# Conditioning rows of up to eight weight chunks summed into one tile and turned into columns four times

## The chip, the cores and the metric

The kernel runs on one core of one Trainium2 chip. The metric is the device time of one execution in microseconds. Engines: PE is TensorE (matmul), PEld its weight load, DVE VectorE, ACT ScalarE, POOL GpSimd, SP SyncE, which here issues the weights' DMAs.

## What is computed

A sequence of 256 tokens with 1024 features goes through a first block (attention, a state-space mixer and a linear recurrence side by side) and then through two decoder layers. Each decoder layer has a front (retention, an RWKV recurrence and a short convolution, merged by gates) and an experts' half (32 experts, two of them chosen for each token). All is float32. The part that matters here is the conditioning of the two decoder layers: one vector `c` of 1024 numbers gives, per layer, six vectors of 1024 by which the layer shifts, scales and gates its activations:

```python
mod = silu(c) @ w_ada[l] + b_ada[l]          # 1024 x 6144, for both layers
h = modulate(rms_norm(x), shift, scale)      # h * (1 + scale) + shift
x = x + gate * branch                        # once for the front, once for the experts
```

## The kernel before

All weights come in chunks of 128x4096 float32 (2 MB), in one fixed order of use that `order` (L399) writes down. `w_ada` is 24 of those chunks, 12 per layer, each for 512 of the 6144 columns; they are set between the other chunks: (0,0) to (0,8) in block 1, (0,9) to (0,11) and (1,0) to (1,4) in the front of layer 0, (1,5) to (1,11) in the front of layer 1. A chunk is written (l,i): layer and number.

SBUF is one large tile, `memory`, and a second one, `parts` (split operands) or `spare` (expert chunks). `Plan` (L224) makes a dry run first, notes at which step each tile and chunk is taken and freed, gives each its columns, and lets each chunk's DMA start as early as its place is free, but in the order of use; `start` (L420) issues it on SP. The chunks' times count steps of the program (a taking or a freeing), so code that takes fewer tiles shifts the table.

Dense projections take float32 weights in two parts: `unit` (L519) makes a high part of 1024 weights per partition on ACT (L522) and a low part on DVE (L523), and `mm3` (L527) multiplies them. Their PE work stands in the profile as `pst<-parts` or `po<-parts`, L505, since one helper `mm` issues nearly all matmuls. A chain of small steps (recurrence, attention, softmax) is written between pieces of dense work by `weave` (L664); the order in which each engine gets its instructions is then set by the tile framework's scheduler, not by the source's order alone.

The conditioning: `spread_c` (L1058) sets silu(c) as the first of 32 columns of a zeroed tile `cs32`. `ada` (L1090) gets a chunk and multiplies it in eight matmuls with 32 weight columns: four partial rows, each a quarter of the features, stand in partitions 0, 32, 64 and 96 of one PSUM bank, with zeros in the others. DVE copies the bank to a tile `r` (L1100). A closure `columns` (L1104) is set aside in `self.side`; `flush` (L1119) runs what waits there at the next `unit` or the next `ada`. It turns the row into columns with the features on partitions: `r`'s slices are the weights and a column of ones is the moving operand, which sums the four partial rows as well. Vectors 3 and 4 (shift and scale of the experts' half) are wanted in another order of features and take every eighth column of `r`, in eight matmuls for 64 partitions each; the others take four matmuls for 128. DVE then adds the bias (L1111 or L1115).

```python
for j in range(8):                                            # vectors 3 and 4
    self.mm(q[o, j:j + 1], r[:, j::8], one, True, True)
...
for j in range(4):                                            # the others
    self.mm(q[:, j:j + 1], r[:, j * 128:(j + 1) * 128], one, True, True)
```

At the end of block 1, `add_x` (L594) adds the sums to x, `inv_rms` (L614) makes the rows' rs with three Newton steps on DVE (L583 to L585), `scale_x` (L621) scales x by it, and `flip` (L628) transposes it on PE (L631) for the front. In an expert's half, chunks for gate, up and down projection (`in_weg`, `in_weu`, `in_wed`) are used in turn.

Of the kernel before, what the change touches and what calls it, by code (L numbers as in the profile page):

```python
# [21 lines left out]
# ---------------------------------------------------------------- host layout  # L22
# [5 lines left out]
def _chunk(w):  # L28
    """[K*128, N] -> [128, K*N], row d = 128*k + p at partition p."""
    kp, n = w.shape  # L30
    return w.reshape(kp // 128, 128, n).transpose(1, 0, 2).reshape(128, -1)


def _rows(v):
    return np.broadcast_to(np.asarray(v).reshape(1, -1), (128, np.asarray(v).size))
# [24 lines left out]
def _constants():  # L60
# [6 lines left out]
    c.add("io32", _rows(np.arange(33, dtype=np.float32)))  # L67
    c.add("io9", _rows(np.arange(8, dtype=np.float32) - 9.0))
# [32 lines left out]
def _layout(inp):  # L101
# [44 lines left out]
    for l in range(2):  # L146
# [19 lines left out]
        lay["ada"].append(np.stack([_chunk(ada[:, i * 512:(i + 1) * 512]) for i in range(12)]))  # L166
# [25 lines left out]
# ---------------------------------------------------------------- the kernel  # L192
class Act:
    """Activations, features on partitions: float32 and its exact two-part split."""
# [5 lines left out]
class Dry:  # L200
    """Stands for anything in the run that only plans the memory."""
# [22 lines left out]
class Plan:  # L224
    """Sizes and lifetimes of all tiles by a dry run, and from them each tile's place and each weight chunk's time to
    start: as early as there is room for it. Times count the steps of the program that take or free memory."""
# [19 lines left out]
    def place(self, first):  # L246
        """An address for every tile, from the bottom, and for every chunk while it is used, from the top: the large
        and long ones first, and before them those that found no room."""
# [28 lines left out]
    def early(self):  # L277
        """Every chunk in turn starts as early as some place is free for it, in the main part or, while that is open
        for chunks, in the other."""
# [26 lines left out]
class Memory:  # L306
    """Columns of one tile, given out and taken back in the order of the program; the waits follow from the data."""
# [6 lines left out]
    def step(self):  # L314
        """One step on; the chunks whose time has come start."""
# [6 lines left out]
    def new(self, *sh, p=128, part=0):  # L322
        """A tile of this shape on the first p partitions."""
# [22 lines left out]
    def chunk(self):  # L346
        """The next weight chunk's number."""
        self.step()
        if self.tiles is None:
            self.plan.chunks.append([Plan.CHUNK, self.now, None, 0])  # L350
        self.got += 1
        return self.got - 1
# [6 lines left out]
    def turn(self, key, *sh, bufs=2, p=128, part=0):  # L359
        """One of bufs tiles of this shape, by turns, until done()."""  # L360
# [11 lines left out]
class Kernel:  # L372
# [26 lines left out]
    def order(self):  # L399
        """The weight chunks in the order in which they are used."""  # L400
# [19 lines left out]
    def start(self, n, t):  # L420
# [4 lines left out]
        # an expert half's last chunk in parts, so that little work is left after the last of them  # L425
# [6 lines left out]
    def get(self, *key, k=8, hold=False):  # L432
        """The next weight chunk; it is there until the next call, or until drop()."""
# [20 lines left out]
    def run(self, plan, dry):  # L454
# [24 lines left out]
        # the last norm: all but the last quarter times its gain before the rows' rs is there  # L479
# [7 lines left out]
    # -- helpers  # L487
    def turn_part(self, spare):
        """The second part of the memory is for split operands, or it is spare and takes weight chunks."""
# [14 lines left out]
    def mm(self, out, lhsT, rhs, start, stop):  # L504
        self.nc.tensor.matmul(out, lhsT=lhsT, rhs=rhs, start=start, stop=stop)  # L505

    def psb(self, tag="sm", name="pst"):
        """A bank of PSUM."""
        return self.ps.tile([128, 512], F, tag=tag, bufs=BANKS[tag], name=name)

    def split(self, f, n=4):
        """f = hi + lo, both exact in the tensor engine's one-pass float32."""
# [6 lines left out]
    def unit(self, src, a, n=1024):  # L519
        """The split of 1024 weights a partition."""  # L520
# [6 lines left out]
    def mm3(self, jobs, left):  # L527
        """out += w.T @ a, or a.T @ w, for every out, w, a, start, stop, from the parts: those with the weights' high
        part first. The product of both low parts is below float32's own rounding."""
# [6 lines left out]
    def fm_pair(self, w, act, m, K=8):  # L536
        """Feature tiles m, m+1 of the projection of act, features on partitions."""
# [10 lines left out]
    def tm(self, w, act):  # L548
        """The projection of act, tokens on partitions: two banks of 128 tokens."""
# [8 lines left out]
    def tm_out(self, w, act, accs, first, last):  # L558
        """accs[t][h] += the projection of four feature tiles of act."""
# [9 lines left out]
    def rsqrt(self, out, in_, scale, eps, tmp):  # L569
        """out = (in_*scale + eps) ** -0.5 on small tiles."""  # L570
# [3 lines left out]
    def newton(self, out, v):  # L574
        """out = v ** -0.5: a first guess from the bits, then three Newton steps; v is overwritten."""
# [11 lines left out]
    def squares(self, t, h):  # L587
        """The mean square of half a row of x, into ss."""
# [5 lines left out]
    def add_x(self, accs, last=False):  # L594
        """x += accs, and its mean squares."""
# [9 lines left out]
    def last_gain(self):  # L605
        """The last norm's gain on every partition."""
# [18 lines left out]
    def flip(self, v, by8, use):  # L625
        """Two feature tiles of v's transpose at a time: use(k, their bank)."""
# [7 lines left out]
    def norm_T(self, gain, shift=None):  # L634
        """The split of x's rms-norm, transposed: uT[d, t] * gain[d] (+ shift[d])."""
# [28 lines left out]
    def weave(chain, dense):  # L664
        """Trace the steps of a chain with pieces of dense work between them."""
# [4 lines left out]
    # -- block 1  # L670
    def block1(self):
# [10 lines left out]
        def softplus(out, x, t):  # L682
            """out = max(x, 0) + log1p(exp(-|x|)); t: four scratch tiles."""
# [15 lines left out]
        # forget gates and time steps, heads on partitions  # L699
# [19 lines left out]
        # token-major dt, exp(cumsum), decay to the chunk's end  # L719
# [14 lines left out]
        def conv(p, raw, out, j, wn, bn, nt):  # L734
            """causal conv of width 4 of psum tile p along time."""
# [1257 lines left out]
```

## Time and profile before

| what | value |
|---|---|
| runs | 1982.15, 1986.38, 1988.5 us; median 1986.38 |
| profiled execution, span from first to last instruction | 1985.8 us (its time is not listed apart from this) |
| PE busy | 1659.6 us, 84% |
| DVE busy | 958.3 us, 48% |
| ACT busy | 557.6 us, 28% |
| DMA, mean | 295 GB/s, 586.13 MB |
| chain that ended last | DMA 19%, PE 3%, all others together under 1% of the span |

Each share is a mean over stages of different kinds. The chain that ended last reaches back only into the last experts' half, so what ends the earlier stages is read from the stages themselves. Busy PE is not PE at its peak: its matmuls are pipelined and their ends modelled, so what an instruction costs is read here from start to start. A float32 matmul of the program stands as two matmuls in the trace, one with the split operands as one.

### The profile page before, as it was taken

The page shows a single profiled execution, that of the slowest core. Times are in us where ns is not written, and L with a number is a line of the kernel's source. Part 1 is how long each engine was busy: PE and PEld are TensorE (multiplying, and loading weights), DVE is VectorE, ACT ScalarE, POOL GpSimd, SP SyncE. Part 2 cuts the span into 40 slices and gives each one's busy share as a digit, 9 for nine tenths or more (in the row PEclk, how much of TensorE's full clock was granted, in tenths as well). Part 3 has the DMA queues.
Part 4 walks back from the last instruction along what each step waited for, and adds up shares of the span by engine and source line. Part 5 has one row for each costly group of instructions (what it writes and reads, how often), then busy time and mean ns, then how long its engine had stood idle before and what let it go on. Part 6 is the DMA issues. An engine that isn't in the chain of part 4 may idle for free. (4 is left out here: it accounts for less than half of the span.)

```text
span 1985.8 us, 42525 instructions
## 1 busy us (share of the span) xinstructions
PE 1659.6 (84%) x18982; PEld 1379.8 (69%) x18982; DVE 958.3 (48%) x2013; ACT 557.6 (28%) x856; POOL 76.6 (4%) x54
## 2 busy tenths in 40 slices
PE   6999999999999887776677599999988877667774
PEld 6877669788988765555455398889987765545553
DVE  7896556788438433222222456784376332222222
ACT  6835444524425300000000235244253100000001
POOL 0001000000004000000000000000040000000000
PEclk9999999999989899888888799999998998788888
DMA  8654563563325799999999953642258999999996
GB/s 344 236 193 155 201 262 131 212 251 132 128 100 234 291 426 426 426 427 425 427 427 426 399 221 133 259 161 105 109 188 324 391 426 425 427 426 426 426 426 252
DMA packets 43119, 586.13 MB, mean 295 GB/s; under 512 B 4816, under 2 KB 5456, under 8 KB 7984
## 3 DMA queue, kind: packets, MB, share of 16 engines
q1 hardware_dynamic: 41904, 579.72, 71.6%
q0 software_dynamic: 1024, 3.61, 0.5%
q8 instruction: 151, 2.47, 0.5%
q14 instruction: 40, 0.33, 0.0%
HBM read 582.26 MB, written 1.05 MB: 294 GB/s over the span
## 5 line engine op out<-in xcount | busy, mean ns | idle before, releaser
L505 PE MATMUL pst<-parts 128*128 128x256 f32 (+2 forms) x4344 | 636.6, 306 | 17.1 <-DVE parts L523 12.4
L505 PEld LDWEIGHTS pst<-parts 128*128 128x128 f32 (+1 forms) x4344 | 578.7, 197 | 65.8 <-issue 17.7
L505 PE MATMUL pst<-memory 128*32 128x256 f32 (+11 forms) x5152 | 519.7, 354 | 83.6 <-DMA memory<-in_wed_dram 43.5
L505 PEld LDWEIGHTS pst<-memory 128*32 128x32 f32 (+5 forms) x5152 | 373.7, 157 | 189.2 <-issue 115.9
L505 PE MATMUL pst<-memory,spare 128*32 128x128 f32 (+1 forms) x6848 | 266.1, 317 | 136.1 <-DMA memory<-in_weu_dram 77.4
L523 DVE TENSOR_TENSOR parts<-memory,parts 128x1024 fp32r<-128x1024 f32 (+1 forms) x233 | 296.7, 1276 | 156.6 <-ACT parts L522 147.6
L522 ACT ACTIVATE parts<-memory 128x1024 fp32r<-128x1024 f32 (+1 forms) x233 | 245.6, 1057 | 425.0 <-PE pst L505 348.1
L505 PEld LDWEIGHTS pst<-memory,spare 128*32 128x32 f32 (+1 forms) x6848 | 237.4, 129 | 178.8 <-issue 117.7
L1886 DVE TENSOR_TENSOR spare<-pst,memory 32x256 f32<-32x256 f32 x256 | 107.6, 420 | 172.0 <-PE pst L505 169.1
L1870 ACT ACTIVATE memory<-pst 128x128 f32<-128x128 f32 x64 | 25.2, 393 | 544.7 <-PE pst L505 525.9
L1872 DVE TENSOR_TENSOR memory<-memory,pst 128x128 f32<-128x128 f32 x64 | 24.0, 375 | 193.8 <-PE pst L505 193.7
L1871 DVE TENSOR_TENSOR memory<-memory,pst 128x128 f32<-128x128 f32 x64 | 24.2, 378 | 193.3 <-ACT memory L1870 193.3
L505 PE MATMUL po<-parts 128*128 128x512 f32 x384 | 89.6, 392 | 2.0 <-ACT parts L515 1.5
L505 PEld LDWEIGHTS po<-parts 128*128 128x128 f32 x384 | 71.5, 188 | 20.6 <-ACT parts L515 3.0
L1822 ACT ACTIVATE spare<-pst,memory,gain 128x128 f32<-128x128 f32 x64 | 29.3, 457 | 189.0 <-DVE spare L1824 189.0
L505 PE MATMUL pst<-spare 128*32 128x128 f32 x1408 | 51.0, 304 | 25.9 <-DMA spare<-in_weu_dram 12.9
L505 PEld LDWEIGHTS pst<-spare 128*32 128x32 f32 x1408 | 45.4, 123 | 32.8 <-issue 26.2
L505 PE MATMUL acc<-spare,memory 128*128 128x512 f32 x128 | 59.8, 610 | 9.2 <-DVE spare L1886 9.2
L1824 DVE TENSOR_SCALAR spare<-pst,gain,memory 128x128 f32<-128x128 f32 x64 | 26.2, 409 | 66.1 <-PE pst L505 56.7
L1291 POOL TENSOR_TENSOR memory<-memory 128x1024 f32<-128x1024 f32 x16 | 47.8, 3019 | 209.8 <-ACT memory L1145 209.8
L505 PEld LDWEIGHTS acc<-spare,memory 128*128 128x128 f32 x128 | 21.8, 189 | 38.1 <-DVE spare L1886 22.8
L505 PE MATMUL pst<-spare,memory 128*32 128x256 f32 x352 | 27.4, 459 | 14.5 <-DMA spare<-in_wed_dram 8.5
(381 smaller groups left out, 974.1 us busy)
## 6 DMA issues: line engine op xcount, KB each, us to landing
memory<-in_weg_dram SPq DMA_DIRECT2D x54, 2048.0 KB, 39.1
memory<-in_weu_dram SPq DMA_DIRECT2D x52, 2048.0 KB, 39.3
memory<-in_wed_dram SPq DMA_DIRECT2D x52, 2048.0 KB, 39.1
memory<-in_w_dram SPq DMA_DIRECT2D x33, 2048.0 KB, 8.6
memory<-in_ada_dram SPq DMA_DIRECT2D x24, 2048.0 KB, 7.6
memory<-in_wg_dram SPq DMA_DIRECT2D x12, 2048.0 KB, 8.2
spare<-in_weu_dram SPq DMA_DIRECT2D x12, 2048.0 KB, 39.1
spare<-in_wed_dram SPq DMA_DIRECT2D x10, 2048.0 KB, 40.5
```

The costliest lines, as they stand in the source:

```text
L505: self.nc.tensor.matmul(out, lhsT=lhsT, rhs=rhs, start=start, stop=stop)
L522: self.nc.scalar.activation(hi, src, AF.Copy)
L523: self.nc.vector.tensor_tensor(lo, src, hi.bitcast(F), op=OP.subtract)
L1291: nc.gpsimd.tensor_tensor(w[:, k], w[:, k], gb, op=OP.mult)
L1822: A.activation(XG[:, j + i, :], p[:, i, :], AF.Identity, scale=gain(j + i), bias=shift(j + i))
L1824: V.tensor_scalar(XG[:, j + i, :], p[:, i, :], gain(j + i), shift(j + i), op0=OP.mult, op1=OP.add)
L1870: A.activation(hf, pg, AF.Sigmoid)
L1871: V.tensor_tensor(hf, hf, pg, op=OP.mult)
L1872: V.tensor_tensor(hf, hf, pu, op=OP.mult)
L1886: V.tensor_tensor(Y[r, s], p[32 * c:32 * c + 32, 0:256], gb[32 * c:32 * c + 32, s], op=OP.mult)
```

## The change

Up to eight chunks share one tile. `cs40` has silu(c) as column 8 of 40, and chunk number n of a group (0 to 7) takes the 32 columns from 8-n on as weights, so that its partial rows stand in partitions n, 32+n, 64+n and 96+n. The first chunk of a group is copied to `rowsum`, every further one is added to it. After chunks (0,3), (0,8), (1,4) and (1,11) the tile is turned: four matmuls with eight moving columns, `sel`, each of which has ones in rows i, 32+i, 64+i and 96+i, and one addition of the bias for each layer in the group. The groups have 4, 5, 8 and 7 chunks. For vectors 3 and 4 the host writes `w_ada`'s columns in the order wanted, so that all chunks are turned alike; the bytes loaded are the same. `mm` is now a property, so that the profile names the caller's line; comments were taken out.

```diff
+    sel = np.zeros((128, 8), np.float32)
+    for i in range(8):
+        sel[i::32, i] = 1.0
+    c.add("sel", sel)
...
+        ada = [a.reshape(D, 128, 8).transpose(0, 2, 1).reshape(D, D) if i in (3, 4) else a for i, a in enumerate(np.split(ada, 6, 1))]
+        lay["ada"].append(np.stack([_chunk(a[:, h * 512:(h + 1) * 512]) for a in ada for h in range(2)]))
...
-        self.cs32 = self.m.new(8, 32)
-        self.nc.gpsimd.memset(self.cs32, 0.0)
-        self.nc.gpsimd.tensor_copy(self.cs32[:, :, 0:1], self.sc[:, :, None])
+        self.cs40 = self.m.new(8, 40)
+        self.nc.gpsimd.memset(self.cs40, 0.0)
+        self.nc.gpsimd.tensor_copy(self.cs40[:, :, 8:9], self.sc[:, :, None])
...
         w = self.get("ada", l, i)
+        n = len(self.rows)
         p = self.psb()
         for m in range(2):
             for c in range(4):
-                self.mm(p[32 * c:32 * c + 32, :], self.cs32[:, 4 * m + c, :], w[:, 4 * m + c, :], m == 0, m == 1)
-        r = self.m.new(512)
-        nc.vector.tensor_copy(r, p)
-        v, h = divmod(i, 2)
-        one = self.C("one")
-
-        def columns():
-            q = self.psb()
-            if v in (3, 4):
-                o = slice(64 * h, 64 * h + 64)
-                for j in range(8):
-                    self.mm(q[o, j:j + 1], r[:, j::8], one, True, True)
-                V.tensor_tensor(self.mod[l][o, 8 * v:8 * v + 8], q[o, 0:8], self.L(l, "bada", 8 * v, 8)[o], op=OP.add)
-            else:
-                for j in range(4):
-                    self.mm(q[:, j:j + 1], r[:, j * 128:(j + 1) * 128], one, True, True)
-                V.tensor_tensor(self.mod[l][:, 4 * i:4 * i + 4], q[:, 0:4], self.L(l, "bada", 4 * i, 4), op=OP.add)
-            self.m.free(r)
-
-        self.side.append(columns)
+                self.mm(p[32 * c:32 * c + 32, :], self.cs40[:, 4 * m + c, 8 - n:40 - n], w[:, 4 * m + c, :], m == 0, m == 1)
+        if n == 0:
+            self.rowsum = self.m.new(512)
+            V.tensor_copy(self.rowsum, p)
+        else:
+            V.tensor_tensor(self.rowsum, self.rowsum, p, op=OP.add)
+        self.rows.append((l, i))
+        if (l, i) in ((0, 3), (0, 8), (1, 4), (1, 11)):
+            self.side.append(self.columns)
+
+    def columns(self):
+        q = self.psb()
+        for j in range(4):
+            self.mm(q[:, 8 * j:8 * j + 8], self.rowsum[:, j * 128:(j + 1) * 128], self.C("sel"), True, True)
+        q = q[:, 0:32].rearrange("p (j i) -> p i j", i=8)
+        for l in range(2):
+            at = [n for n, r in enumerate(self.rows) if r[0] == l]
+            if at:
+                s = slice(4 * self.rows[at[0]][1], 4 * self.rows[at[-1]][1] + 4)
+                o = self.mod[l][:, s].rearrange("p (i j) -> p i j", j=4)
+                b = self.L(l, "bada", s.start, s.stop - s.start).rearrange("p (i j) -> p i j", j=4)
+                self.nc.vector.tensor_tensor(o, q[:, at[0]:at[-1] + 1, :], b, op=OP.add)
+        self.m.free(self.rowsum)
+        self.rows = []
```

How the instructions move on PE, in the front of layer 0, where chunks (0,11) and (1,0) are turned. Before (`32x512` is a chunk's row, `128x1` its columns, `parts` dense work):

```order
L505 MATMUL pst<-memory 32x512 x8
L505 MATMUL pst<-parts 128x256 x9
L505 MATMUL pst<-memory 128x1 x4
L505 MATMUL pst<-parts 128x256 x30
L505 MATMUL pst<-memory 128x512 x2
L505 MATMUL pst<-parts 128x256 x48
L505 MATMUL pst<-memory 32x512 x8
L505 MATMUL pst<-parts 128x256 x24
L505 MATMUL pst<-memory 128x1 x4
```

The same place in the changed kernel (L1107 is the row; the dense work is split in L539 and L541, the jobs with the high and the low part of the weights):

```order
L1107 MATMUL pst<-memory 32x512 x8
L539 MATMUL pst<-parts 128x256 x7
L541 MATMUL pst<-parts 128x256 x8
L539 MATMUL pst<-parts 128x256 x16
L541 MATMUL pst<-parts 128x256 x8
L1427 MATMUL pst<-memory 128x512 x2
L539 MATMUL pst<-parts 128x256 x16
L541 MATMUL pst<-parts 128x256 x8
L539 MATMUL pst<-parts 128x256 x16
L541 MATMUL pst<-parts 128x256 x8
L1107 MATMUL pst<-memory 32x512 x8
```

The rows stay where they stood; the blocks of columns are gone, and only dense work lies between the rows.

The seam between block 1 and the front of layer 0, on PE. Before: the rest of w_out's projection, the rows and columns of chunk (0,9), the row of (0,10), the transposes of L631, and the columns of (0,10):

```order
L505 MATMUL po<-parts 128x512 x48
L505 MATMUL pst<-memory 32x512 x3
L505 MATMUL pst<-memory 64x1 x8
L505 MATMUL pst<-memory 32x512 x8
L631 MATMUL pst<-memory 128x128 x16
L505 MATMUL pst<-memory 128x1 x4
L505 MATMUL pst<-parts 128x256 x384
```

And in the changed kernel, where the transposes are L638:

```order
L539 MATMUL po<-parts 128x512 x4
L541 MATMUL po<-parts 128x512 x2
L1107 MATMUL pst<-memory 32x512 x8
L638 MATMUL pst<-memory 128x128 x16
L1107 MATMUL pst<-memory 32x512 x3
L539 MATMUL pst<-parts 128x256 x16
```

The eight matmuls ahead of the transposes are the last three of chunk (0,9) and the first five of chunk (0,10); the last three of (0,10) follow the transposes.

On SP the chunks' DMAs, from the first two dense chunks of layer 0's front on (`in_w` is a dense chunk). Before:

```order
L429 DMA memory<-in_w_dram 128x4096 x2
L429 DMA memory<-in_ada_dram 128x4096 x2
L429 DMA memory<-in_w_dram 128x4096 x2
L429 DMA memory<-in_ada_dram 128x4096 x2
L429 DMA memory<-in_w_dram 128x4096 x2
```

Now:

```order
L435 DMA memory<-in_w_dram 128x4096 x2
L435 DMA memory<-in_ada_dram 128x4096
L435 DMA memory<-in_w_dram 128x4096
L435 DMA memory<-in_ada_dram 128x4096
L435 DMA memory<-in_w_dram 128x4096 x3
L435 DMA memory<-in_ada_dram 128x4096 x3
```

Chunk (0,10) now comes after the third dense chunk, into the place of w_out's last chunk, and chunk (0,11) after the sixth, where it came after the fourth.

## Rows read from the trace of the kernel before

**Rows 1.** The page's slices of 49.6 us: granted clock and DMA share, in tenths.

```profile
PEclk9999999999989899888888799999998998788888
DMA  8654563563325799999999953642258999999996
```

**Rows 2.** Busy by stage: PE, PEld, DVE, ACT, POOL, granted clock, DMA share, GB/s.

```profile
50.00:291.00 241.00, 237.74 (x1362) 183.24 (x1360) 170.80 (x351) 127.73 (x202) 13.72 (x13) 0.97 0.55 204
303.00:662.00 359.00, 347.60 (x3083) 313.31 (x3084) 237.84 (x365) 150.35 (x193) 28.14 (x12) 0.97 0.47 179
692.00:1120.00 428.00, 300.22 (x5294) 232.47 (x5286) 109.22 (x300) 27.78 (x67) 1.57 (x4) 0.89 1.01 425
1142.00:1517.00 375.00, 361.06 (x3155) 324.53 (x3155) 236.71 (x365) 150.92 (x196) 26.81 (x11) 0.96 0.48 182
1542.00:1970.00 428.00, 310.58 (x5358) 238.20 (x5350) 109.23 (x300) 30.09 (x70) 0.00 (x0) 0.86 0.99 418
```

**Rows 3.** Groups by form on PE: busy us, mean ns, idle before, its releasers.

```profile
L505 PE MATMUL pst<-memory 128*128 128x1 f32 x128 | 16.6, 251 | 2.3 <-DVE memory L1100 2.1
L505 PE MATMUL pst<-memory 128*64 128x1 f32 x128 | 16.6, 259 | 2.9 <-DVE memory L1100 2.6 <-DVE memory L1215 0.3
```

**Rows 4.** Timeline of PE at a block of four: start, length, count.

```profile
64.05 0.95 PE L505 MATMUL pst<-memory 128*128 128x1 f32 x8
64.86 0.36 PE L505 MATMUL pst<-parts 128*128 128x256 f32 x1
```

**Rows 5.** Timeline of PE at a block of eight.

```profile
1205.50 2.05 PE L505 MATMUL pst<-memory 128*64 128x1 f32 x16 [0.28 <-DVE memory L1215]
1207.49 0.86 PE L505 MATMUL pst<-parts 128*128 128x256 f32 x3
```

**Rows 6.** Timeline of PE at the seam of block 1 and front 0.

```profile
293.37 4.77 PE L505 MATMUL pst<-memory 128*64 128x1 f32 x32 [1.96 <-DVE memory L1100]
298.25 2.67 PE L631 MATMUL pst<-memory 128*128 128x128 f32 x16
300.76 0.95 PE L505 MATMUL pst<-memory 128*128 128x1 f32 x8
```

**Rows 7.** Timeline of DVE at the same seam.

```profile
295.48 0.17 DVE L1111 TENSOR_TENSOR memory<-pst,memory 64x8 f32<-64x8 f32 x1 [1.52 <-PE pst L505]
```

**Rows 8.** Groups by form on DVE, columns as in rows 3.

```profile
L1100 DVE COPY memory<-pst 128x512 f32<-128x512 f32 x24 | 16.5, 688 | 4.6 <-PE pst L505 4.5
...
L1253 DVE TENSOR_TENSOR memory<-memory,pst 128x512 f32<-128x512 f32 x8 | 5.5, 687 | 40.5 <-PE pst L505 40.5
...
L1111 DVE TENSOR_TENSOR memory<-pst,memory 64x8 f32<-64x8 f32 x8 | 1.3, 163 | 13.9 <-PE pst L505 13.9
```

**Rows 9.** Timeline of SP's DMA issues in front 0.

```profile
291.46 23.39 SPq L429 DMA_DIRECT2D memory<-in_ada_dram  x2
326.04 11.85 SPq L429 DMA_DIRECT2D memory<-in_w_dram  x2
```

**Rows 10.** DMA issues: count, KB each, median us to landing.

```profile
memory<-in_ada_dram SPq DMA_DIRECT2D x24, 2048.0 KB, 7.6
```

**Rows 11.** Timeline of DVE: the copy of chunk (0,11).

```profile
362.65 0.68 DVE L1100 COPY memory<-pst 128x512 f32<-128x512 f32 x1
```

**Rows 12.** Stretches of 3.4 us on PE: busy (matmuls), granted clock, DMA share, GB/s.

```profile
214.40:217.80 3.40, 3.40 (x8) 0.50 0.08 17
234.90:238.30 3.40, 3.40 (x17) 0.50 0.00 0
...
1207.70:1211.10 3.40, 3.40 (x17) 0.50 0.00 0
1228.20:1231.60 3.40, 3.40 (x18) 0.50 0.11 48
1231.60:1235.00 3.40, 3.40 (x31) 1.00 0.03 5
1248.60:1252.00 3.40, 3.40 (x18) 0.51 1.00 429
```

## What was predicted

> **What bounds the kernel now.** I read the page's slices first, then the busy time by stage, then the chain at work inside a stage, and last the conditioning's own instructions. The slices show the DMA engines at 9 tenths in two long stretches, which are the experts' halves, and well below that elsewhere [rows 1]. By stage: in block 1 (50 to 291 us) PE is busy 237.74 of 241 us, in the two fronts 347.60 of 359 and 361.06 of 375, with DMA at a share of about a half; in the two experts' halves DMA stands at 1.01 and 0.99 with 425 and 418 GB/s, and PE at some 70% [rows 2]. So the first stage and both fronts last as long as PE's queue, and the experts' halves as long as their weights take. All 24 conditioning chunks lie in block 1 and the fronts. The experts' stream can only start when a front gives its memory free, so a front that ends earlier moves the whole stream forward; microseconds taken off PE there should reach the end one for one.
>
> **What goes.** Before, each of 24 chunks is turned into columns on its own: 16 times four matmuls with 128 weight columns and one moving column, 8 times eight with 64. Each program matmul stands as two in the trace, 128 of either kind [rows 3]. What such a block keeps from PE is the time from its first start to the start of the next dense matmul. For a block of four that is 64.86 - 64.05 = 0.81 us [rows 4], for one of eight 1207.49 - 1205.50 = 1.99 us [rows 5]. Sixteen of the first are 13.0 us, eight of the second 15.9 us. In front of them PE was idle 2.3 + 2.9 = 5.2 us, nearly all of it until the copy of L1100 was done [rows 3]. Together 34.1 us.
>
> Not all of it is on the path. At the seam between block 1 and the first front PE has nothing but conditioning to do: the blocks of chunks (0,9) and (0,10) lie where the transposes of L631 wait for the norm. There 1.96 us of wait, 2.0 us of the block and 0.81 us of the other, 4.8 us, are covered by the chain of small DVE operations that makes the row's rs [rows 6]. That chain has its own share: DVE, which works in order, stood 1.52 us until PE had made the columns of (0,9), with the Newton steps queued behind [rows 7]. Without that addition the steps go on; but the new order puts a weight split among them, so I bound the gain between 0 and 1.5 us and take 0.5. This leaves 34.1 - 4.8 + 0.5 = 29.8 us.
>
> **What comes.** Four blocks of four matmuls with eight moving columns. No row has eight; the nearest are the blocks with one: 0.81 us for the same four weights [rows 4], at worst the 1.99 us of the block with twice as many [rows 5]. I take 0.81, since the weights loaded are the same, so 3.2 us. (The Trainium skill, TensorE: Matmul & The Clock Gate, Back-to-back issue gap, gives one price to a matmul of 1 to 64 moving columns; no run here shows it yet, and by it the price would also be the lower one.) Each block waits for the last partial row, as before: between 0 and 1.96 us [rows 6]; the mean of the 24 is 5.2 / 24 = 0.22, so 0.9 us in all. Together 4.1 us; at the upper ends of both 4 x (1.99 + 1.96) = 15.8.
>
> **What is moved or swapped for nothing.** Twenty copies of 128x512 out of PSUM become additions of the same size: 688 against 687 ns [rows 8], and no one on PE waits for them any more but at the four turns. The row's matmuls stay eight per chunk with 32 weight columns, only the place of the nonzero column differs. The 24 small additions on DVE become 5; DVE loses with them the 13.9 us that it stood before the eight of L1111 [rows 8]; I count no gain for it, since PE and not DVE ends these stages. POOL's memset of 320 instead of 256 columns lies long before its first use. The rewoven order of PE, DVE and ACT holds the same dense matmuls.
>
> SP: the planner lets eleven chunks of the two fronts start with one chunk fewer ahead, since fewer steps and other addresses free their places later. I cost it at nothing, and the cover is this: chunk (0,11) is the second issue of the row at 291.46, at 314.5 us [rows 9], lands 7.6 us later, at 322 [rows 10], and is copied out at 362.65 [rows 11], so it lies ready for some 38 us. A place freed one chunk later costs about 11.5 us, the distance of the two issues at 326.04 [rows 9]. At the seam chunk (0,10) now goes into the place of the last chunk of w_out. Its five matmuls stand ahead of the transposes: if they are late, so are those; the transposes wait until 298.25 anyway [rows 6].
>
> **The clock.** Something that the blocks do behind them is larger than their wait. In the 3.4 us after five of the 64-wide blocks the granted clock is 0.50 of full speed, 1.2 instead of 2.4 GHz: from 214.4, 234.9, 1207.7, 1228.2 and 1248.6 us [rows 12]. Before 1207.7 PE had been without work for no more than the 0.28 us in front of that block [rows 5]. The stretch from 1228.2 holds 18 matmuls, the next, at full clock, 31 of mostly the same dense form [rows 12]: 3.4 x (1 - 18/31) = 1.4 us lost, five times 7.0 us. I take it that the eight single-column matmuls bring the fall, and that a block of four with eight columns does not, since none of the five falls follows a block of four. That the falls follow these blocks is read from the rows; that they cause them is my choice.
>
> The Trainium skill speaks against this term: the same page, Why this matters for your kernels, puts a falling clock down to stretches in which TensorE is idle between bursts of matmuls. The trace does not agree, as the 0.28 us shows. By that rule the falls would not be the blocks' and would stay, which is the first rival.
>
> **The sum.** 29.8 - 4.1 + 7.0 = 32.7 us off a profiled span of 1985.8 us gives 1953.1. The median of the runs shown is 1986.38, 0.6 above that span; I say 1953.
>
> **The rivals.**
> (1) The clock falls stay. For it: the attention's narrow matmuls stand near two of the five, and a stretch at low clock also holds other work. Against it: three of the five stand in plain dense work with nothing but the block before them. Then 29.8 - 4.1 = 25.7 us go: 1960.
> (2) The new order of the instructions opens gaps. All of PE's idle time in the three PE-bound stages is 3.3 + 11.4 + 13.9 = 28.6 us [rows 2]; if the rewoven queues had half as much again, 14 us would be given back: 1967. Against it: the dense work is long and can be placed freely.
> (3) The time is hidden: the stages are set by something else (DVE's splits, the chunks' arrival), and PE's freed time becomes waiting. For it: DVE is busy 170.80 of 241 us in block 1, and 237.84 of 359. Against it: that is two thirds, and PE's own idle time there is 1 to 4% [rows 2]. Then 1986, no change.
> (4) Slower, by late chunks. SP issues in order, so one chunk whose place is freed late holds all behind it. If PE came to stand for the whole landing time at each of the eleven chunks, 11 x 7.6 = 84 us would come and 32.7 go: 2037. It turns the sign from 3.0 us per chunk on. Against it: 38 us of lead less 11.5 us.
> That the change does not do what it says can be set aside: the order shows four blocks where 24 stood.
>
> **How the numbers follow.** Forecast 0.68, (1) 0.16, (2) 0.06, (3) 0.06, (4) 0.04. The likeliest case at its best has the full 1.5 us at the seam and no new waits: 34.1 - 4.8 + 1.5 - 3.2 + 7.0 = 34.6; with the runs' own scatter (the lowest is 4.2 under the median) and a clock fall or two more that go at 1.4 us each, some 10 us under 1953: low 1943. High: the falls stay and half of the new blocks' extra 11.7 us is paid, 1960 + 6 = 1966. About 0.3% is what a measurement of this kernel can tell from no change, 6 us: forecast, (1) and (2) are faster by more than that, 0.90; (3) is the 0.06; (4) the 0.04.
>
> **What will show it.** In the profile after: single-column matmuls gone, 32 trace matmuls with eight columns, each turn 0.8 us from its start to the next dense start; PE's wait for L1100 down to four turns; full clock where it fell in the middle of the second front (now some 25 us earlier); each PE-bound stage shorter by about 10 us, the experts' halves unchanged in length. The forecast is wrong if those falls are still there at other places, if PE waits for DMA inside a front, or if a stage's idle time grew.

## The result and the profile after

The changed kernel takes 1958.11 us (median of four runs, 1956.24 to 1962.8) against 1986.37 (four runs, 1982.15 to 1988.5): ratio 0.9865, 95% interval 0.9848 to 0.9882, 28.3 us less. A second measurement with more rounds, further down, gives 0.9867 (0.985 to 0.9883). The profiled execution took 1956.24 us, the lowest of the four, with a span of 1954.5 us.

The page's slices after, which answer to [rows 1]:

```profile
PEclk9999999999999899877889799999998999888988
DMA  8643754672335799999999956733357999999995
```

The shape is the same: two long stretches at 9 tenths of DMA, which are the experts' halves, and less elsewhere.

Busy time by stage after, columns as in [rows 2] (PE, PEld, DVE, ACT, POOL, granted clock, DMA share, GB/s):

```profile
50.00:283.00 233.00, 221.97 (x1270) 170.63 (x1271) 167.82 (x341) 125.82 (x200) 14.50 (x13) 0.99 0.55 201
295.00:650.00 355.00, 343.35 (x3043) 309.77 (x3045) 237.52 (x362) 150.20 (x193) 27.55 (x12) 0.97 0.50 187
680.00:1108.00 428.00, 304.88 (x5294) 235.34 (x5290) 109.06 (x300) 27.66 (x66) 1.63 (x4) 0.87 1.01 425
1130.00:1484.00 354.00, 344.53 (x3067) 309.37 (x3069) 234.51 (x358) 151.00 (x196) 26.97 (x11) 0.98 0.52 191
1510.00:1938.00 428.00, 299.70 (x5342) 232.50 (x5338) 109.24 (x300) 30.43 (x70) 0.00 (x0) 0.90 0.99 418
```

The experts' halves are untouched, at 425 and 418 GB/s. In block 1 PE's busy time fell by 237.74 - 221.97 = 15.8 us, but the stage became only some 8 us shorter: its idle time rose from 3.3 to 233 - 221.97 = 11.0 us. In the first front it stayed at 11.6 against 11.4, in the second it fell from 13.9 to 9.5.

How long a stage lasts can be taken between the first transposes of each stage (L631 before, at 13.13, 298.25, 663.88, 1133.78 and 1515.93 us; L638 after, at 12.37, 289.96, 651.67, 1121.28 and 1483.65 us):

| stage | before | after | change |
|---|---|---|---|
| block 1 | 285.1 us | 277.6 us | -7.5 |
| front 0 | 365.6 | 361.7 | -3.9 |
| experts 0 | 469.9 | 469.6 | -0.3 |
| front 1 | 382.1 | 362.4 | -19.7 |
| experts 1 to the end | 469.9 | 470.8 | +0.9 |

The turns, grouped by form on PE (columns as in [rows 3]), and one of them in PE's timeline (as [rows 4]):

```profile
L1120 PE MATMUL pst<-memory 128*128 128x8 f32 x32 | 3.9, 249 | 0.2 <-DVE memory L1112 0.2
```

```profile
234.52 0.95 PE L1120 MATMUL pst<-memory 128*128 128x8 f32 x8
235.33 0.94 PE L539 MATMUL po<-parts 128*128 128x512 f32 x3
```

A turn with eight moving columns takes 235.33 - 234.52 = 0.81 us, the same as with one [rows 4]; the four waited 0.2 us together. The Trainium skill (TensorE: Matmul & The Clock Gate, Back-to-back issue gap) gives one price from 1 to 64 moving columns; the trace agrees for one and for eight, 0.81 us either way.

Granted clock right behind two of the turns (busy PE, matmuls, clock, DMA share, GB/s), which answer to [rows 12]:

```profile
235.30:238.70 3.40, 3.40 (x17) 1.00 0.94 399
1250.10:1253.50 3.40, 3.40 (x30) 1.00 0.92 390
```

Full clock: all five falls of [rows 12] are gone.

Where block 1 gave some of it back, PE's timeline:

```profile
93.10 1.97 PE L539 MATMUL pst<-parts 128*128 128x512 f32 x8
100.67 1.65 PE L541 MATMUL pst<-parts 128*128 128x512 f32 x3 [5.60 <-DVE parts L530]
```

PE stood 5.60 us for one weight split. DVE's timeline in that time:

```profile
94.94 1.22 DVE L895 TENSOR_TENSOR memory<-memory 128x1024 f32<-128x1024 f32 x1
...
96.45 0.69 DVE L897 TENSOR_TENSOR_SCAN memory<-memory 128x256 f32<-128x256 f32 x1
...
98.66 0.69 DVE L897 TENSOR_TENSOR_SCAN memory<-memory 128x256 f32<-128x256 f32 x1
...
99.39 1.23 DVE L530 TENSOR_TENSOR parts<-memory,parts 128x1024 fp32r<-128x1024 f32 x1
```

The four scans of a recurrence (L897) and small Newton steps stand ahead of the split (L530), while PE has nothing else. In the kernel before, a split stood ahead of the scans (L890 there), at 97.77 us:

```profile
97.77 1.22 DVE L523 TENSOR_TENSOR parts<-memory,parts 128x1024 fp32r<-128x1024 f32 x1
...
100.78 0.69 DVE L890 TENSOR_TENSOR_SCAN memory<-memory 128x256 f32<-128x256 f32 x1
```

From 99.5 us on, still within the wait, the clock is low for two stretches:

```profile
99.50:102.90 3.40, 2.23 (x5) 0.50 0.00 0
102.90:106.30 3.40, 3.40 (x9) 0.50 0.45 87
```

This fall comes 4.4 us after PE became idle, at 95.07 us, unlike the five falls of [rows 12].

At the seam, PE, SP and DVE:

```profile
286.84 3.19 PE L1107 MATMUL pst<-memory 128*32 128x512 f32 x10 [3.22 <-DMA memory<-in_ada_dram]
289.96 2.29 PE L638 MATMUL pst<-memory 128*128 128x128 f32 x16
```

```profile
278.67 0.33 SPq L435 DMA_DIRECT2D memory<-in_ada_dram  x1
```

```profile
286.29 1.23 DVE L530 TENSOR_TENSOR parts<-memory,parts 128x1024 fp32r<-128x1024 f32 x1
...
288.80 0.75 DVE L629 TENSOR_SCALAR memory<-memory,rs 128x1024 f32<-128x1024 f32 x1
```

Chunk (0,10) is asked for at 278.67 and PE waits 3.22 us for it; but the norm, with the split among its steps, ends only at 288.80 + 0.75 = 289.55, so the transposes, which start at 289.96, could have started at most 0.4 us sooner.

### The profile page after: what moved, and what is told of

The parts are those of the page before. It is cut to its first block, busy times and chain, and to the rows that moved or that the text cites. A ratio compares the mean times of both kernels' runs of the same rounds, so it can differ in the third digit from the quotient of the medians.

```text
span 1954.5 us, 42045 instructions
## 1 busy us (share of the span) xinstructions
PE 1618.7 (83%) x18754; PEld 1344.8 (69%) x18758; DVE 955.0 (49%) x1994; ACT 557.5 (29%) x856; POOL 76.9 (4%) x54
## 5 line engine op out<-in xcount | busy, mean ns | idle before, releaser
L539 PE MATMUL pst<-parts 128*128 128x256 f32 (+2 forms) x2896 | 455.5, 306 | 5.4 <-DVE parts L663 4.0
L539 PEld LDWEIGHTS pst<-parts 128*128 128x128 f32 (+1 forms) x2896 | 396.4, 197 | 47.1 <-issue 16.9
L1878 PE MATMUL pst<-memory,spare 128*32 128x128 f32 x6784 | 258.1, 317 | 146.4 <-DMA memory<-in_weu_dram 81.3
L530 DVE TENSOR_TENSOR parts<-memory,parts 128x1024 fp32r<-128x1024 f32 (+1 forms) x233 | 297.7, 1281 | 160.4 <-ACT parts L529 155.1
L1878 PEld LDWEIGHTS pst<-memory,spare 128*32 128x32 f32 x6784 | 230.0, 128 | 189.0 <-issue 128.8
L541 PE MATMUL pst<-parts 128*128 128x256 f32 (+2 forms) x1448 | 236.7, 301 | 20.1 <-DVE parts L530 19.9
L541 PEld LDWEIGHTS pst<-parts 128*128 128x128 f32 (+1 forms) x1448 | 202.1, 195 | 30.6 <-DVE parts L530 24.1
L1894 PE MATMUL pst<-memory 128*32 128x256 f32 x1696 | 119.4, 429 | 58.2 <-DMA memory<-in_wed_dram 41.5
L1894 PEld LDWEIGHTS pst<-memory 128*32 128x32 f32 x1696 | 60.1, 120 | 102.5 <-issue 59.4
L1831 PE MATMUL pst<-memory 128*128 128x128 f32 x512 | 126.0, 408 | 0.6 <-DVE memory L1825 0.6
L1831 PEld LDWEIGHTS pst<-memory 128*128 128x128 f32 x512 | 123.0, 334 | 4.2 <-issue 3.5
L1878 PE MATMUL pst<-spare 128*32 128x128 f32 x1408 | 48.8, 294 | 23.5 <-DMA spare<-in_weu_dram 11.4
L539 PE MATMUL po<-parts 128*128 128x512 f32 x256 | 65.4, 393 | 2.0 <-ACT parts L522 1.5
```

What stands on the lines that cost most here:

```text
L530: self.nc.vector.tensor_tensor(lo, src, hi.bitcast(F), op=OP.subtract)
L539: self.mm(out, *((w[0], a[n]) if left else (a[n], w[0])), start and n == 0, False)
L541: self.mm(out, *((w[1], a[0]) if left else (a[0], w[1])), False, stop)
L1831: self.mm(p[:, i, :], self.x[:, t, j + i::8], S[:, t].rearrange("p e s -> p (e s)"), t == 0, t == 1)
L1878: self.mm(ps[-1][32 * c:32 * c + 32, :], XG[:, j, s], w[:, j, 128 * c:128 * c + 128], j == 0, j == 7)
L1894: self.mm(p[32 * c:32 * c + 32, 0:256], h4[:, j, :], wd[:, j, 256 * c:256 * c + 256], j == 0, j == 3)
```

## Experiments

Two theories were open after this. What made a block of eight (the eight matmuls with 64 weight columns each) dear, and brought the half clock: eight matmuls of one column in a row, the narrow weights, or the reading of every eighth element? And was the wait at 100.67 us a price of the change, or would PE have stood a little later in any case?

### Every chunk turned alone

```diff
-        if (l, i) in ((0, 3), (0, 8), (1, 4), (1, 11)):
+        if True:
```

> Every chunk is turned into columns on its own again, but all 24 in the form with four matmuls and eight moving columns: no sums, no block of eight. Theory (the blocks of eight cost 1.99 - 0.81 us more than those of four, and the five stretches at half clock are theirs): twenty turns more than the changed kernel, 20 x 0.81 = 16.2 us, with waits of up to 0.22 us each (4.4), of which about 3 us lie under the norm's chain at the seam: 1958 + 13 to 18 = 1971 to 1976 us, and no stretch at half clock at the five places. Rival (the falls belong to turning a chunk alone, in whatever form): five stretches more, 7 us: 1978 to 1983, each right behind a turn.

Measured: 1974.14 us, ratio to before 0.9942 (0.9924 to 0.9959), within the theory. Its turns on PE:

```profile
L1120 PE MATMUL pst<-memory 128*128 128x8 f32 x192 | 24.6, 254 | 3.8 <-DVE memory L1110 3.5 <-DVE memory L1227 0.3
```

None of the five falls is there. So by this run 16 us of the change lie in the grouping (twenty turns at 0.81 us and 3.6 us of waits, less what the seam covers), and 12 us in what remains when nothing is grouped. The five falls don't belong to turning a chunk alone. One turn does have the half clock right behind it, from 176.2 us, but ahead of it stands a row of small matmuls behind which other runs have a fall as well (the kernel before from 170.0 us, still within that row). A wait for a split in block 1 is there too, 3.94 us at 102.49, where the changed kernel has two, 7.9 us in all; so the division into 16 and 12 holds only to some 4 us.

### Blocks of eight added to the changed kernel

```diff
+        if i // 2 in (3, 4):
+            self.side.append(lambda: self.extra(i % 2))
+
+    def extra(self, h):
+        q, o = self.psb(), slice(64 * h, 64 * h + 64)
+        for j in range(8):
+            self.mm(q[o, j:j + 1], self.x[:, 0, j:512:8], self.C("one"), True, True)
```

> The changed kernel with eight blocks of eight matmuls added, 64 weight columns and one moving column each, on data that is always ready, at the chunks where the kernel before had such blocks; nothing reads their result. Theory (a block of eight keeps PE for 1.99 us, and the clock falls behind it): 8 x 1.99 = 15.9 us and some five falls at 1.4 us, 7.0: 1958 + 23 = 1981 us, stretches at half clock right behind the blocks. Rival 1 (the falls came from the work around them): 15.9 us alone, 1974, no stretch behind a block. Rival 2 (PE's time there is not what ends the stages): 1958 to 1960.

Measured: 1977.38 us, 19.3 over the changed kernel, between the theory and rival 1. The trace decides: six of the eight blocks have the half clock right behind them. One of them in PE's timeline, and the stretches behind it:

```profile
1202.19 2.08 PE L1122 MATMUL pst<-memory 128*64 128x1 f32 x16
1204.20 1.10 PE L539 MATMUL pst<-parts 128*128 128x256 f32 x7
```

```profile
1205.30:1208.70 3.40, 3.40 (x18) 0.51 1.01 429
1208.70:1212.10 3.40, 3.40 (x21) 0.99 0.04 14
```

The block takes 2.01 us, on data that had long been there and with no idle time ahead of it. Against the changed kernel, the dense matmuls start 2.1 us later behind the first block, which has no fall behind it, and 3.5 us later behind each of the first three blocks of the second front, which have one: a fall costs 1.4 to 1.5 us. The block at the seam cost nothing, since it lies in a wait there.

### The same with 128 weight columns, and both with neighbouring columns

Three variants of the added block; only the weights' slice (and with 128 the output's partitions) changes.

```diff
-            self.mm(q[o, j:j + 1], self.x[:, 0, j:512:8], self.C("one"), True, True)
+            self.mm(q[:, j:j + 1], self.x[:, 0, j:1024:8], self.C("one"), True, True)
```

> As the run with eight added blocks of eight, but with 128 weight columns in each matmul, one moving column; nothing reads their result. Eight such matmuls are two blocks of four: 2 x 0.81 = 1.6 us each, 13.0 in all. Theory A (the falls follow from eight matmuls of one column in a row, whatever the weights' width): stretches at half clock behind these blocks too, 1958 + 13 + 7 = 1978 us. Theory B (they follow from the half-wide weights): no such stretches, 1971 us.

```diff
+            self.mm(q[:, j:j + 1], self.x[:, 0, 128 * j:128 * j + 128], self.C("one"), True, True)
```

> As the run with eight added blocks of eight 128-wide matmuls (3.8 us a block in its trace), but the weights are 128 neighbouring columns of the tile where that run took every eighth; nothing reads the result. Theory (what costs is that a weight load takes every eighth element): 16 trace matmuls at 0.81 / 8 = 0.10 us, 1.6 us a block, 13 in all, and no stretch at half clock behind the blocks: 1958 + 13 = 1971 us. Rival 1 (the price is that of eight one-column matmuls in a row): 3.8 us a block again and the half clock too, 1998 us. Rival 2 (the price is the stride's, the clock is the row of eight's): 13 + five to eight falls at 1.4 us, 1978 to 1982 us.

```diff
+            self.mm(q[o, j:j + 1], self.x[:, 0, 64 * j:64 * j + 64], self.C("one"), True, True)
```

> As the run with eight added blocks of eight 64-wide matmuls (2.01 us a block in its trace, half clock behind six of them), but the weights are 64 neighbouring columns where that run took every eighth; nothing reads the result. Theory (the stride costs): at most 16 x 0.10 = 1.6 us a block, 13 in all, no half clock behind: 1966 to 1971 us. Rival (64-wide matmuls of one column cost as such): 2.0 us a block and the falls again, 1977 us.

| weights of the added block | columns | us a block | behind it | time, us |
|---|---|---|---|---|
| every eighth element | 64 | 2.01 | half clock behind 6 of 8 | 1977.38 |
| every eighth element | 128 | 3.8 | half clock behind 8 of 8, one of them at the seam | 1998.20 |
| neighbours | 128 | 1.8 | full clock behind 7 | 1966.97 |
| neighbours | 64 | 1.02 | full clock behind 7 | 1962.08 |

With neighbours, the eighth block is the one at the seam, where the changed kernel has a fall of its own behind the waits; away from the seam the counts are 6 of 7, 7 of 7, none of 7 and none of 7. The two runs with neighbours came out faster than I had expected (1971, and 1966 to 1971). The ratios to before are 1.0066 (1.0048 to 1.0083), 0.9911 (0.9888 to 0.9934) and 0.9874 (0.9857 to 0.989) for the last three. The weight loads by form (busy us, mean ns, idle before), of the run with every eighth element and of that with neighbours, 128 columns each:

```profile
L1122 PEld LDWEIGHTS pst<-memory 128*128 128x128 f32 x128 | 31.0, 334 | 4.2 <-issue 1.7 <-ACT memory L1431 0.8 <-DVE memory L607 0.8
```

```profile
L1122 PEld LDWEIGHTS pst<-memory 128*128 128x128 f32 x128 | 14.9, 192 | 4.2 <-issue 1.7 <-DVE memory L1460 0.8 <-DVE memory L607 0.8
```

Granted clock behind a block of the first, then of the second:

```profile
1217.20:1220.60 3.40, 3.40 (x17) 0.50 0.88 366
```

```profile
1199.20:1202.60 3.40, 3.40 (x30) 1.00 0.92 386
```

So the price is the stride's, and neither the number of one-column matmuls nor the narrow weights bring the falls: theory B falls with the first of these runs, where wide weights have them, and theory A with the other two, where eight one-column matmuls in a row have none. Both had the price wrong too: 3.8 us a block are far over the 1.6 that I took from contiguous weights. The Trainium skill (Advanced Engine Details and Errata, SBUF Cachelines) says that accesses which each fall into another 16-byte line are penalised, and that the tolerated stride depends on the type. Eight float32 are 32 bytes, so the rows agree, 334 against 192 ns. The page gives no price for it.

For the clock the runs show less. The strided blocks have the falls, but they are also the longer ones, 2.01 and 3.8 us against 1.02 and 1.8; a row of neighbouring weights that lasts as long was not tried. And a stride is not needed: in both fronts of all thirteen profiles the clock also falls in or right behind one row of small matmuls whose weights are neighbours, without idle time ahead. In the changed kernel's first front that row (L1545 and L1546 by turns) runs for 5.6 us, its weight loads take 188 ns, and the clock halves behind it. From PE's timeline, its weight loads, and the stretches in it and behind it:

```profile
544.24 0.33 PE L1545 MATMUL pst<-memory 128*128 128x64 f32 x2
...
549.22 0.43 PE L1545 MATMUL pst<-memory 128*128 128x64 f32 x2
```

```profile
L1545 PEld LDWEIGHTS pst<-memory x16: 186/188/192, 544.1 to 549.3; 128*128 128x128 f32 x16
```

```profile
546.60:550.10 3.50, 3.50 (x24) 1.00 0.00 0
550.10:553.50 3.40, 3.40 (x18) 0.50 0.00 0
```

So taking the stride away takes the falls behind these blocks away; whether through the reading itself or through the shorter block stays open.

The kernel before showed the stride's price already, in a group that I had not read: weight loads of 128 columns by form in the first experts' half (692 to 1120 us), where the gather (L1831 of the kernel after) takes every eighth column of x.

```profile
L505 PEld LDWEIGHTS pst<-memory 128*128 128x128 f32 x224 | 54.0, 335 | 1.7 <-issue 1.7
```

### The host's layout alone, on the kernel before

```diff
-        lay["ada"].append(np.stack([_chunk(ada[:, i * 512:(i + 1) * 512]) for i in range(12)]))
+        ada = [a.reshape(D, 128, 8).transpose(0, 2, 1).reshape(D, D) if i in (3, 4) else a for i, a in enumerate(np.split(ada, 6, 1))]
+        lay["ada"].append(np.stack([_chunk(a[:, h * 512:(h + 1) * 512]) for a in ada for h in range(2)]))
...
-            if v in (3, 4):
...
-            else:
-                for j in range(4):
+            for j in range(4):
```

> The kernel before with the host's part of the change alone: w_ada's columns for vectors 3 and 4 written in the order wanted, so that all 24 chunks are turned by four matmuls of 128 neighbouring weight columns, each on its own, with one moving column. Theory (the block of eight costs because each weight load takes every eighth element, in price and in clock): 8 x (1.99 - 0.81) = 9.4 us and five falls of 1.4 to 1.5 us, 7.0 to 7.5, go: 1986 - 16.7 = 1969 to 1970 us, if the order on DVE in block 1 stays as it was. Rival 1 (the falls are not the blocks'): 1977. Rival 2 (the gain is that of the grouping alone): 1986.

Measured: 1968.20 us, ratio 0.9918 (0.9904 to 0.9932), 17.7 us under before; the expected 16.7 and a little more. Where 2 us of a block and the half clock stood before [rows 5, 12], PE's timeline and the stretch behind:

```profile
1211.76 1.05 PE L506 MATMUL pst<-memory 128*128 128x1 f32 x8 [0.53 <-DVE memory L1101]
1212.68 6.60 PE L506 MATMUL pst<-parts 128*128 128x256 f32 x53
```

```profile
1212.70:1216.10 3.40, 3.40 (x30) 1.00 0.53 227
```

More than half of the change's 28 us is this: two lines of host layout and one form of turn for all chunks, with nothing grouped. In block 1 the split stands ahead of the scans here; the run with every chunk turned alone, in which it waits behind them (3.94 us on PE), was 6 us slower, against times of the kernel before that were alike (1985.82 and 1985.86).

### The order on DVE in block 1

One more step of the interleaving ahead of the scans, so that the scheduler puts three splits ahead of them; the arithmetic is the same.

```diff
             V.memset(th[:, :, 0:1], 1.0)
             yield
+            yield
```

> The changed kernel with one more step of the interleaving ahead of the recurrence's scans, so that on DVE three weight splits (L530) stand ahead of the four scans in block 1, and no longer behind them. Theory (PE's 5.60 us wait at 100.67 us is the new order on DVE, and the half clock at 99.5 us follows from it): the wait goes, block 1 ends 5 to 8 us earlier, and the time is 1950 to 1953. Rival (DVE has the same work either way, PE stands for the same splits a few us later): block 1 as long as before this edit, 1957 to 1960 us.

Measured: 1952.12 us, ratio 0.9836 (0.9817 to 0.9855). PE at the same place:

```profile
96.60 1.20 PE L541 MATMUL pst<-parts 128*128 128x512 f32 x4 [1.12 <-DVE parts L530]
97.63 1.99 PE L539 MATMUL pst<-parts 128*128 128x512 f32 x8
```

and DVE:

```profile
95.33 1.22 DVE L530 TENSOR_TENSOR parts<-memory,parts 128x1024 fp32r<-128x1024 f32 x1
...
96.84 1.22 DVE L530 TENSOR_TENSOR parts<-memory,parts 128x1024 fp32r<-128x1024 f32 x1
...
100.71 0.68 DVE L898 TENSOR_TENSOR_SCAN memory<-memory 128x256 f32<-128x256 f32 x1
```

The wait is 1.12 us in place of 5.60, no half clock follows, and block 1 lasts 270.4 us in place of 277.6 (in the second pair, below, 273.2 in place of 278.0). The difference to the changed kernel is only some six microseconds, so both were run again on one chip.

> The changed kernel once more, on the same chip as the two runs beside it and with more rounds: 1956 to 1960 us, 28 us under the kernel before.

> The changed kernel with the step ahead of the scans once more. Theory (5.60 us of wait were DVE's order): 5 to 7 us under the changed kernel beside it, 1951 to 1953. Rival (the 6 us were the scatter between two calls): the same as it, within 2 us.

Measured: 1957.56 us (0.985 to 0.9883 of before) and 1949.86 us (0.981 to 0.9837). The intervals don't touch; the step is worth 7.7 us there, 6.0 in the first pair. This is the fastest kernel of the study, 36 us under the one before.

The step on the kernel before, without the change:

> The kernel before, with only the step ahead of the recurrence's scans added; nothing of the change. Theory (the wait of 5.60 us in block 1 is one that the change's order made; the kernel before has none there, since its split stands ahead of the scans already): no gain, 1983 to 1989 us. Rival (the step is worth 6 us in any order): 1980 us, and then the change by itself was worth 28 us and nothing was given back.

Measured: 1984.91 us, ratio 0.9988 (0.9976 to 0.9999): 2.8 us under the kernel before, within the theory's range. Where they are from is not shown. PE's idle time in block 1 is no less. The stretch at half clock from 170.0 to 176.8 us of the kernel before is absent, but a fall near that place comes and goes between executions of one kernel: the changed kernel with the step has none in its first profile and one from 167.9 us in its second. So of the 6 to 8 us on the changed kernel some 3 to 5 are the change's own loss, and up to 3 come from the step in any order.

### Three turns in place of four

```diff
-        if (l, i) in ((0, 3), (0, 8), (1, 4), (1, 11)):
+        if (l, i) in ((0, 7), (1, 3), (1, 11)):
```

> The changed kernel with the step ahead of the scans (1952 us by itself) and three turns in place of four, after the chunks (0,7), (1,3) and (1,11). Theory (a turn is its 0.81 us and little else): 1951 us, within the scatter of 1952. Rival (a turn also stands in the order that the scheduler makes, and its place matters): up to 5 us either way, 1947 to 1957.

Measured: 1963.77 us, ratio 0.9903 (0.9874 to 0.9932): one turn less, and 12 us more than the kernel with four. The rival was right in kind, and its 5 us too small. Block 1 lasts 280.7 us against 270.4; PE in it:

```profile
183.92 1.63 PE L1006 MATMUL pst<-memory 128*128 128x128 f32 x4 [3.25 <-DVE rsy L592]
187.48 1.97 PE L1015 MATMUL pst<-memory 128*128 128x64 f32 x8 [1.92 <-ACT memory L1010]
```

```profile
184.00:197.70 13.70, 11.78 (x44) 0.50 0.07 20
```

Two waits, and 13.7 us at half clock around and behind them, at a place where no turn stands. That here too the scheduler ordered the small chains and the dense work otherwise fits this, but I did not follow the order itself. The first experts' half is longer as well, 475.1 us against 472.4.

## Why the prediction was right, and where not

1. **The blocks that go.** 34.1 us, of which 4.8 covered, was right in the main: the layout alone and the grouping alone each gave about what their blocks cost (17.7 us measured for 16.7; 16 for the twenty turns). Together these would be 33.7, while the change gave 28.3; the losses of point 4 can account for the difference. The price of 0.81 us for all sixteen blocks of four was a little low: in PE's timeline most take 0.81 to 0.91, and the one at 170.62 us, in a stretch at half clock, 1.73. At the seam I took 0.5 us. The row matmuls ahead of it start at 290.35 before and at 282.56 after, 7.79 us earlier, the transposes 8.29 us earlier [rows 6]: 0.50 us.

2. **The blocks that come.** 4.1 us forecast, 3.5 measured: 4 x 0.81 and, at one turn, 0.1 more, with waits of 0.2 instead of 0.9. The lower bound was the right one. "No row has eight" overlooked a nearer row than the one used: in the kernel before, eight trace matmuls with 128 weight columns and 64 moving ones took 210.82 - 210.01 = 0.81 us.

```profile
210.01 1.00 PE L505 MATMUL pst<-memory 128*128 128x64 f32 x8
210.82 0.71 PE L505 MATMUL pst<-parts 128*128 128x512 f32 x2
```

3. **The clock.** 7.0 us for five falls: all went, and a fall costs 1.4 to 1.5 us where blocks of eight are put back. That the blocks cause them, which was my choice, is shown, and rejects rival (1). What I blamed in them was wrong: eight single-column matmuls bring no fall when their weights are neighbours. Read with a stride they do, at blocks twice as long; which of the two it is stays open. The Trainium skill (TensorE: Matmul & The Clock Gate, Why this matters for your kernels) lays a falling clock to idle time between bursts of matmuls: the fall at 99.5 us, in the wait of 5.60 us, agrees with it; the falls behind the added blocks and the one at 550.1 us, with no idle time ahead of them, don't.

4. **The step that failed** is the one costed at nothing: "The rewoven order of PE, DVE and ACT holds the same dense matmuls." It does, but not in an order that feeds PE as well. The wait of 5.60 us, one of 2.31 us at 164.85 and the low clock behind the first were rival (2) in small; mending the order gave 6.0 and 7.7 us, of which up to 2.8 came without the change too. The text named the sign, "if a stage's idle time grew", and it grew from 3.3 to 11.0 us in block 1.

5. **What came unforeseen on the other side.** In the second front the kernel before waited 1.49 us at 1243.70 for a split; 0.52 us are left of it. A wait of 0.78 us at 1254.55 is gone, and of two among small matmuls at 1336 and 1340, 3.57 us together, one of 1.85 is left. With these 3.5 us, the parts of the second front's 19.7 us that I can name come to some 18; the rest was not followed. The half clock from 170.0 to 176.8 us is absent too, but that changes between executions of one kernel. These gains and the loss of point 4 pull in opposite directions, so part of how close the sum came is luck: the profiled execution's span, 1954.5, is 1.4 us over the 1953.1 of the sum, and the median, 1958.11, 5 us over it.

6. **By stage** the text said some 10 us each. Its own rows gave it unevenly: six small blocks only in front 0, four of the eight large ones and three falls in front 1. Measured were 7.5, 3.9 and 19.7.

7. Rival (3), hidden time, is rejected: the experts' halves kept their length to 1 us and started as much earlier as the fronts had become shorter. Rival (4) stayed a single wait of 3.22 us for chunk (0,10), covered by the norm but for at most 0.4 us; that was read from the trace and not tried.

## What to carry to other kernels

Look at the weight loads by form before counting matmuls: a stationary operand read with a stride cost up to twice its price here, with lost clock behind the blocks, and a layout prepared on the host removed both without any grouping. Where a scheduler weaves small chains between dense work, an edit elsewhere can shuffle them, so cost "the same work in another order" at a few microseconds either way, and compare idle time stage by stage afterwards. Fewer instructions are not a reason by themselves: three turns were slower than four.

## What the hardware showed that was not expected

- A float32 weight load of 128 columns took 334 ns with every eighth element and 192 ns with neighbours. From start to start a block of sixteen trace matmuls took 3.8 against 1.8 us, and with 64 columns 2.01 against 1.02 us.
- Behind such blocks the granted clock went to 0.50 (1.2 GHz) for 3.4 to 6.8 us, though PE was not idle ahead of them. Away from the seam it fell behind six of seven blocks with 64 columns, all seven with 128, and none of the fourteen with neighbouring columns.
- The same fall, also without idle time, came at 550.1 us behind 5.6 us of small matmuls with neighbouring weights. What these have in common with the strided blocks stays open.
- Eight moving columns cost what one costs: 0.81 us a turn, 0.91 at one of the four.
